# All 16 z blocks in the seven-product pair stage, and the decay of the decode states moved there through DRAM

## The chip, the cores and the metric

The kernel runs on one core of a Trainium2 chip. The metric is the device time of one execution in microseconds. The kernel before has a median of 2105.8 us over 3 runs (2105.5 to 2109.59).

## The reference, cut to what matters

One inference step of a hybrid decoder layer: 1024 tokens of a new prompt, and 8 sequences that are decoded by one token each (T = 1032 columns in the kernel). One input projection gives z, the inputs x, B and C of a state-space mixer (SSD), a pooling input and two gates.

```python
xn = rms_norm(x, p['norm_mix_pre'])
proj = xn @ p['w_in']
z, xbc, dt_raw, u_pool, gate_a, gate_b = jnp.split(proj, idx, axis=-1)
xbc_c, conv_new = causal_conv(xbc, conv_prev, p['conv_w'], p['conv_b'])
xs, bm, cm = jnp.split(xbc_c, [D_INNER, D_INNER + N_GROUPS * D_STATE], axis=-1)
y, ssm_new = ssd_scan(xs, dt, a, bm, cm, ssm_prev)
y = y + p['d_skip'][:, None] * xs
y_a = rms_norm(y * jax.nn.silu(z), p['ssm_norm'])
y_b, pool_new = pool_mix(u_pool, pool_prev, start_pos, p['w_pool_group'], p['pool_scale'])
merged = jax.nn.sigmoid(gate_a) * (y_a @ p['w_branch_a']) + jax.nn.sigmoid(gate_b) * (y_b @ p['w_branch_b'])
h = x + rms_norm(merged @ p['w_out'], p['norm_mix_post'])
gu = rms_norm(h, p['norm_ffn_pre']) @ p['w_ffn_in']
g, up = jnp.split(gu, [D_FF], axis=-1)
f = (jax.nn.silu(g) * up) @ p['w_ffn_out']
out = h + rms_norm(f, p['norm_ffn_post'])
```

For a token of the decoded sequences the scan is one step: the stored state times exp(dt a), plus dt x B, and the output is that state times C. The width of the model is 1024, of z and x 2048 each (16 blocks of 128 rows), and there are 8 groups of SSD heads, each with one block of B, one of C, two of x and two of z.

## The kernel before, in words

Rows of a block lie on the 128 partitions, and tokens along the free axis, in thirds of 344 columns. All products are of float32 quality: each operand is split into a high and a low part, and a product is three matmuls (high by high, high by low, low by high; `mm3`, L260 to L262). The normed input stays on chip as `xh` and `xl`. A weight block comes from DRAM by SP's DMA queue (`wr`), ScalarE casts it to its high part (`wh`, L194), and VectorE subtracts for the low part (`wl`, L195). All weights stand in one plan (`plan_weights`); two loads are kept ahead, and one split is made ahead of its use (`w_dma`, `w_split`, `load_w`). The instructions of each engine are laid out by a scheduler, so their order is not that of the text.

The stages are these. First the pooling branch's projections. Then the **pair stage** (about 146 to 377 us): 22 blocks of the input projection, as 11 pairs, each computed as a product of 2 by 2 blocks in seven products in place of eight. The list `PAIRS` names them: `ga` and `gb` are gate blocks, `z0` to `z3` eight of the 16 z blocks. `prep1` makes the weight operands of a product, three products ahead (`RING`); `product1` runs its 24 matmuls of 258 columns (L710 to L712) and adds the result into rows of the pair (copies L715 and L719, additions L717 to L727). `finish_pair` applies tanh, for z multiplies (L748, L749), and stores the block to DRAM (L750, `s_z`).

Then the **group stage** (about 377 to 1011 us). `group_proj(g)` computes five blocks of group g as direct products: B, C, x0 and x1, each followed by the causal convolution (`conv`: first tap L733 on ScalarE, three taps L735 on VectorE, tanh L736 on ScalarE, multiply L737 on VectorE), and then one z block (`z_proj`, tanh L880 and multiply L881). Beside it runs `ssd(g-1)`, the scan of the group before, in 8 chunks of 128 tokens: per chunk four products into a bank `T` (L916 to L919: transposes of B, x0, x1, and B by C), from which VectorE makes `xdt`, `wx` and `CB` (L924 to L928) and the decay matrix `E` (L935); then the state product into a bank `S` (L948), the state's part of the output (L950), the output product `y` (L960), the state's update `hT` (multiply L967 on GpSimd, addition L968 on VectorE), the state's part times its decay (`eA`, L971), and the sum in `Y` (L976 on VectorE, L980 on GpSimd). Beside the chunks stand the decode steps: load a state (`st`), `dx` (L999), GpSimd's product of B and `dx` (L1001), the decay multiply (L1002), the addition of both (L1006), GpSimd's product with C (L1008), VectorE's reduction (L1012, `ys`). At the end come Y times z (L1033), the store of Y, and the sum of its squares. `interleave` takes 0.585 steps of the SSD to each step of the projection:

```python
    for _ in group_proj(0):
        pass
    for g in range(1, G):
        interleave(group_proj(g), ssd(g - 1), 0.585)
```

The group stage ends with `gates`, beside which the last scan, `ssd(7)`, runs: two gate blocks, then the first quarter of the branch product, whose operand is the stored Y of groups 0 and 1, loaded as `qr` and split into `qh` (ScalarE) and `ql` (VectorE, L1068). The later stages (the rest of the branch products, the output product, the FFN) are not touched by the change.

## Time and profile before

| | before |
|---|---|
| median of 3 runs | 2105.8 us (2105.5 to 2109.59) |
| the profiled execution, its own time | 2109.54 us |
| its span, first to last instruction | 2107.8 us |
| mean granted TensorE clock | 0.991 of full speed |
| TensorE busy | 98% of the span |
| VectorE, ScalarE, GpSimd busy | 69%, 39%, 18% |
| bytes moved by DMA | 256.48 MB, 122 GB/s on average |

A busy share says for which part of the span an engine had an instruction in work. Times of single instructions are those of this one execution. The table by stretches gives the same shares for a part of the span; the lists of groups give the number of instructions of one line and shape, their busy time, the mean length of one, and the idle time of the engine just before them with what ended it; a timeline shows single instructions in order of their start.

### The profile page before, as it was taken

To read this page: it belongs to the slowest core of one execution; us is meant where nothing else is said; L and a number is where in the kernel's file an instruction comes from. 1 tells how busy PE (TensorE), PEld (TensorE's weight loads), DVE (VectorE), ACT (ScalarE), POOL (GpSimd) and SP (SyncE) were. 2 spreads that over 40 slices of the span, in tenths; PEclk is the share of its full clock that TensorE was granted. 3 is DMA by queue.
4 is the path that set the end of the run, shared out by engine and by line. 5 is a ranking of instruction groups with operands and counts; after the bars stand their busy time and mean duration, and the time that the engine had idled before them with its cause. 6 is when DMAs were issued, how large, how long until landed. Compare 5 with 4: busy or idle time off the path is not lost.

```text
span 2107.8 us, 37452 instructions
## 1 busy us (share of the span) xinstructions
PE 2056.8 (98%) x14986; PEld 2031.3 (96%) x14986; DVE 1457.1 (69%) x2455; ACT 825.0 (39%) x1573; POOL 386.6 (18%) x405
## 2 busy tenths in 40 slices
PE   6999999999999999999999999989999999999997
PEld 5999999999999999999999999989999999999997
DVE  7867555468987898887447773769776766654436
ACT  5353433435554555554422024444333323341112
POOL 3100000024345344435100002451000000000004
PEclk9999999999999999999999999989999999999999
DMA  4333332434344444446515454143232222352133
GB/s 168 89 114 96 111 114 90 136 107 154 124 158 155 150 144 149 153 137 221 199 40 165 147 177 132 61 141 116 88 99 71 91 71 81 117 175 71 43 101 109
DMA packets 126574, 256.48 MB, mean 122 GB/s; under 512 B 25408, under 2 KB 63424, under 8 KB 126400
## 3 DMA queue, kind: packets, MB, share of 16 engines
q1 hardware_dynamic: 125968, 253.80, 37.5%
q8 instruction: 118, 1.93, 0.4%
q14 instruction: 56, 0.46, 0.1%
q10 hardware_dynamic: 432, 0.28, 0.0%
HBM read 195.72 MB, written 58.32 MB: 121 GB/s over the span
## 4 chain that ended last, share of the span: by engine, by line
PE 91%; DVE 5%; ACT 1%; issue 1%; POOL 1%; DMA 0%; ACTq 0%; DVEq 0%; POOLq 0%
PE pj L260 22%; PE pj L261 22%; PE pj L262 22%; PE dj L712 3%; PE dj L710 3%; PE dj L711 3%; PE y L960 2%; PE S L948 1%; PE S L950 1%; PE y L260 1%; PE y L262 1%; PE y L261 1%; PE T L260 1%; PE T L262 1%; PE T L261 1%
## 5 line engine op out<-in xcount | busy, mean ns | idle before, releaser
L260 PE MATMUL pj<-xh,wh 128*128 128x344 f32 x1200 | 393.4, 330 | 3.2 <-ACT xh L330 2.4
L261 PE MATMUL pj<-xl,wh 128*128 128x344 f32 x1200 | 385.0, 321 | 0.1
L262 PE MATMUL pj<-xh,wl 128*128 128x344 f32 x1200 | 383.6, 320 | 0.0
L194 ACT CAST wh<-wr 128x1024 fp32r<-128x1024 f32 (+1 forms) x119 | 123.3, 1037 | 386.0 <-PE pj L261 353.8
L260 PEld LDWEIGHTS pj<-xh,wh 128*128 128x128 f32 x1200 | 225.7, 189 | 9.4 <-issue 5.8
L261 PEld LDWEIGHTS pj<-xl,wh 128*128 128x128 f32 x1200 | 226.3, 189 | 1.7 <-DVE xl L331 0.8
L262 PEld LDWEIGHTS pj<-xh,wl 128*128 128x128 f32 x1200 | 226.3, 189 | 0.0
L1198 POOL TENSOR_TENSOR ssacc<-ssacc,sq 128x258 f32<-128x258 f32 (+3 forms) x41 | 42.9, 1051 | 927.5 <-ACT sq L1197 919.3
L195 DVE TENSOR_TENSOR wl<-wr,wh 128x1024 fp32r<-128x1024 f32 (+1 forms) x104 | 132.0, 1270 | 113.3 <-ACT wh L194 102.6
L261 PE MATMUL pj<-ql,wh 128*128 128x344 f32 (+1 forms) x608 | 191.3, 315 | 2.7 <-DVE ql L1068 2.7
L260 PE MATMUL pj<-qh,wh 128*128 128x344 f32 (+1 forms) x608 | 192.2, 316 | 1.4 <-ACT m L1144 1.4
L262 PE MATMUL pj<-qh,wl 128*128 128x344 f32 (+1 forms) x608 | 190.9, 314 | 0.0
L261 PE MATMUL pj<-al,wh 128*128 128x344 f32 (+2 forms) x528 | 169.1, 320 | 0.0
L260 PE MATMUL pj<-ah,wh 128*128 128x344 f32 (+2 forms) x528 | 168.9, 320 | 0.0
L262 PE MATMUL pj<-ah,wl 128*128 128x344 f32 (+2 forms) x528 | 168.8, 320 | 0.0
L735 DVE SCALAR_TENSOR_TENSOR S<-U,hcw,S 128x1056 f32<-128x1056 f32 x96 | 129.6, 1350 | 1.9 <-ACT S L733 1.7
L1453 DVE TENSOR_TENSOR acc<-acc,pj 128x344 f32<-128x344 f32 (+2 forms) x120 | 60.8, 510 | 98.4 <-PE pj L262 98.2
L261 PEld LDWEIGHTS pj<-ql,wh 128*128 128x128 f32 x608 | 115.7, 190 | 2.9 <-DVE ql L1068 2.9
L260 PEld LDWEIGHTS pj<-qh,wh 128*128 128x128 f32 x608 | 115.1, 189 | 2.4 <-ACT m L1144 1.9
L262 PEld LDWEIGHTS pj<-qh,wl 128*128 128x128 f32 x608 | 115.5, 190 | 0.0
L932 ACT ACTIVATE E<-E,acT 128x128 f32<-128x128 f32 x256 | 85.4, 392 | 50.3 <-DMA E<-s_ac 50.3
L261 PEld LDWEIGHTS pj<-al,wh 128*128 128x128 f32 x528 | 99.2, 188 | 0.0
(438 smaller groups left out, 5950.8 us busy)
## 6 DMA issues: line engine op xcount, KB each, us to landing
wr<-wi SPq DMA_DIRECT2D x61, 512.0 KB, 4.0
E<-s_ac SPq DMA_DIRECT2D x64, 256.0 KB, 3.8
wr<-wfi SPq DMA_DIRECT2D x30, 512.0 KB, 3.6
s_act<-wk SPq DMA_DIRECT2D x44, 258.0 KB, 2.0
ar<-s_act SPq DMA_DIRECT2D x22, 516.0 KB, 4.5
wu<-wfi SPq DMA_DIRECT2D x22, 512.0 KB, 3.6
wr<-wfo SPq DMA_DIRECT2D x20, 512.0 KB, 3.6
s_y<-Y SPq DMA_DIRECT2D x16, 516.0 KB, 4.1
```

The lines of the kernel that those rows point to most:

```text
L194: act.copy(out=wh, in_=raw)
L195: eng.tensor_tensor(out=wl, in0=raw, in1=wh, op=ALU.subtract)
L260: pe.matmul(out, wh, xh, start=start, stop=False)
L261: pe.matmul(out, wh, xl, start=False, stop=False)
L262: last_mm[0] = pe.matmul(out, wl, xh, start=False, stop=stop)
L710: pe.matmul(o, wh_, h[:, cs], start=first and k == 0, stop=False, skip_group_check=True)
L711: pe.matmul(o, wh_, l[:, cs], start=False, stop=False, skip_group_check=True)
L712: pe.matmul(o, wl_, h[:, cs], start=False, stop=k == 3, skip_group_check=True)
L735: dve.scalar_tensor_tensor(out=S[:, :CW], in0=U[:, k:k + CW], scalar=tap(k), in1=S[:, :CW], op0=ALU.mult, op1=ALU.add)
L932: act.activation(out=E[:, h], in_=E[:, h], func=AF.Relu, scale=-1.0, bias=acT[:, c, 4 * g + h:4 * g + h + 1])
L1198: eng.tensor_tensor(out=sacc[:, sl], in0=sacc[:, sl], in1=q, op=ALU.add)
L1453: dve.tensor_tensor(out=acc[ob][:, sl], in0=acc[ob][:, sl], in1=pt, op=ALU.add)
```

## The change

Four pairs are added to the pair stage, so that all 16 z blocks are computed there and stored (`s_z` gets a second half). A z pair now holds the same half of two neighbouring groups' z: pairs z0 to z3 the first block of groups 0 to 7, z4 to z7 the second. `z_proj` and `group_proj` fall away, and with them the z weights in the groups' plan; the groups run the four conv blocks alone, and `ssd` loads both z rows. The new generator `decay` loads a decode state, multiplies it by its decay and stores it to DRAM (`s_st`); it is called from the 17th product of the pair stage on, in two of every five steps. `decode` loads the multiplied state and has no multiply. The ratio of `interleave` goes from 0.585 to 0.73. The line numbers of the new kernel are one lower than before up to the pair stage and two higher in the SSD.

```diff
-PAIRS = "ga0 ga1 z0 ga2 z1 ga3 gb0 z2 gb1 z3 gb2".split()
+PAIRS = "ga0 ga1 z0 ga2 z4 ga3 gb0 z1 gb1 z5 gb2 z2 z6 z3 z7".split()
...
         if kind == "z":
-            return WZ + 4 * n + 1, WZ + 4 * n + 3
+            return WZ + 4 * (n % 4) + n // 4, WZ + 4 * (n % 4) + n // 4 + 2
...
-            want(("in", WZ + 2 * g), wi[WZ + 2 * g])
...
-    s_z = dram.tile([G, P, T], F32, name="s_z")
+    s_z = dram.tile([2, G, P, T], F32, name="s_z")
+    s_st = dram.tile([16, P, NS, P], F32, name="s_st")
...
+    def decay(hp):
+        st = row(1024, name="st").rearrange("p (b n) -> p b n", n=P)
+        sync.dma_start(out=st, in_=sssm[hp])
+        yield
+        dve.tensor_tensor(out=st, in0=st, in1=b4x(dts[:, 1, hp * 8:hp * 8 + 8], P), op=ALU.mult)
+        sync.dma_start(out=s_st[hp], in_=st)
+        yield
...
+        if i >= 16 and (i - 16) % 5 in (0, 4):
+            if (i - 16) % 5 == 0 and len(dec) < 16:
+                dec.append(decay(len(dec)))
+            if dec:
+                next(dec[-1], None)
...
-    def z_proj(g):
-        d = grp[g]
-        wt = load_in(WZ + 2 * g)
-        Z = row(name="Z")
-        d["z0"] = Z
-        for th in range(3):
-            pt = yield from in_half(wt, th)
-            act.activation(out=Z[:, TH[th]], in_=pt, func=AF.Tanh, scale=0.5)
-            dve.scalar_tensor_tensor(out=Z[:, TH[th]], in0=Z[:, TH[th]], scalar=1.0, in1=pt,
-                                     op0=ALU.add, op1=ALU.mult)
-            yield
...
-                sync.dma_start(out=v3(st), in_=sssm[hp])
+                sync.dma_start(out=v3(st), in_=s_st[hp])
...
-                dve.tensor_tensor(out=v3(st), in0=v3(st), in1=b4x(dts[:, 1, hp * 8:hp * 8 + 8], P), op=ALU.mult)
...
             if u == 13:
-                d["z1"] = row(name="Z")
-                sync.dma_start(out=d["z1"], in_=s_z[g])
+                for a in range(2):
+                    d[f"z{a}"] = row(name="Z")
+                    sync.dma_start(out=d[f"z{a}"], in_=s_z[a, g])
...
-    for _ in group_proj(0):
+    for _ in conv_proj(0):
         pass
     for g in range(1, G):
-        interleave(group_proj(g), ssd(g - 1), 0.585)
+        interleave(conv_proj(g), ssd(g - 1), 0.73)
```

The new layout moves instructions at three places.

The first is VectorE at the passage from one group to the next, where the last conv of group g (block x1) and the last chunks of `ssd(g-1)` meet. Names: `S` and `U` are the conv's rows (also the bank `S` of the state product in rows of `hT` and `eA`), `pj` a projection bank, `y` the bank of the output product. Before:

```order
L935 TENSOR_TENSOR E<-E,CB 128x512
L737 SCALAR_TENSOR_TENSOR S<-U,S 128x1056
L881 SCALAR_TENSOR_TENSOR Z<-Z,pj 128x344
L968 TENSOR_TENSOR hT<-hT,S 128x256
L971 TENSOR_TENSOR eA<-eA,S 128x2x128
L968 TENSOR_TENSOR hT<-hT,S 128x256
L881 SCALAR_TENSOR_TENSOR Z<-Z,pj 128x344
L971 TENSOR_TENSOR eA<-eA,S 128x2x128
L976 SCALAR_TENSOR_TENSOR Y<-S,ppt,y 128x256 x2
L1033 TENSOR_TENSOR Y<-Y,Z 128x1032 x2
L195 TENSOR_TENSOR wl<-wr,wh 128x1024
L924 TENSOR_TENSOR xdt<-T,dtT 128x256
```

And after the change:

```order
L970 TENSOR_TENSOR hT<-hT,S 128x256
L973 TENSOR_TENSOR eA<-eA,S 128x2x128
L194 TENSOR_TENSOR wl<-wr,wh 128x1024
L735 SCALAR_TENSOR_TENSOR S<-U,hcw,S 128x1056
L978 SCALAR_TENSOR_TENSOR Y<-S,ppt,y 128x256
L735 SCALAR_TENSOR_TENSOR S<-U,hcw,S 128x1056
L978 SCALAR_TENSOR_TENSOR Y<-S,ppt,y 128x256
L735 SCALAR_TENSOR_TENSOR S<-U,hcw,S 128x1056
L1035 TENSOR_TENSOR Y<-Y,Z 128x1032 x2
L737 SCALAR_TENSOR_TENSOR S<-U,S 128x1056
L926 TENSOR_TENSOR xdt<-T,dtT 128x256
L928 TENSOR_TENSOR wx<-T,wend 128x256
```

The conv's last multiply (L737) stood seven rows ahead of the Y by Z pair and now stands behind it, and the conv's taps lie among the last rows of the scan.

The second is TensorE where the scan of group g begins: the transpose of the decode samples (`ident,bcs`) and the four products of the first chunk. Before they stand together, behind the z block:

```order
L262 MATMUL pj<-xh,wl 128x344
L903 MATMUL T<-ident,bcs 16x128
L916 MATMUL T<-ident,S 128x128
L917 MATMUL T<-ident,S 128x128
L918 MATMUL T<-ident,S 128x128
L919 MATMUL T<-S 128x128
L260 MATMUL pj<-xh,wh 128x344
```

After the change they stand in two pieces, the first behind 24 matmuls of the next group's block B, the second 33 such matmuls (32 in the first and the last group) further on:

```order
L261 MATMUL pj<-xh,wl 128x344
L905 MATMUL T<-ident,bcs 16x128
L918 MATMUL T<-ident,S 128x128
L919 MATMUL T<-ident,S 128x128
L259 MATMUL pj<-xh,wh 128x344
```

```order
L261 MATMUL pj<-xh,wl 128x344
L920 MATMUL T<-ident,S 128x128
L921 MATMUL T<-S 128x128
L259 MATMUL pj<-xh,wh 128x344
L260 MATMUL pj<-xl,wh 128x344
```

The transpose of x1 (L920, before L918) thus comes 57 projection matmuls behind the conv block x1's own last matmul, where before it came behind the 72 of the z block.

The third is VectorE near the end of the group stage, where the splits of the first quarter (`ql`) stand among the rows of `ssd(7)`. Before:

```order
L1068 SCALAR_TENSOR_TENSOR ql<-qr,ppt,qh 128x1032
L999 TENSOR_TENSOR dx<-S,dts 128x8
L1002 TENSOR_TENSOR st<-st,dts 128x1024
L968 TENSOR_TENSOR hT<-hT,S 128x256
L971 TENSOR_TENSOR eA<-eA,S 128x2x128
L976 SCALAR_TENSOR_TENSOR Y<-S,ppt,y 128x256 x2
L1006 TENSOR_TENSOR st<-st,tmp 128x1024
L1068 SCALAR_TENSOR_TENSOR ql<-qr,ppt,qh 128x1032 x2
L924 TENSOR_TENSOR xdt<-T,dtT 128x256
```

And after the change:

```order
L1001 TENSOR_TENSOR dx<-S,dts 128x8
L1070 SCALAR_TENSOR_TENSOR ql<-qr,ppt,qh 128x1032
L970 TENSOR_TENSOR hT<-hT,S 128x256
L973 TENSOR_TENSOR eA<-eA,S 128x2x128
L1007 TENSOR_TENSOR st<-st,tmp 128x1024
L978 SCALAR_TENSOR_TENSOR Y<-S,ppt,y 128x256 x2
L1013 TENSOR_REDUCE ys<-tmp 128x8
L1070 SCALAR_TENSOR_TENSOR ql<-qr,ppt,qh 128x1032 x2
L926 TENSOR_TENSOR xdt<-T,dtT 128x256
```

The reduction of the decode product (L1013, before L1012) stood behind the last two splits and now stands ahead of them; the decay multiply (L1002) is gone, and the second split stands behind `dx`.

## Rows read from the trace of the kernel before

**Rows 1.** The page's first part: busy time, share of the span, number of instructions.

```profile
PE 2056.8 (98%) x14986; PEld 2031.3 (96%) x14986; DVE 1457.1 (69%) x2455; ACT 825.0 (39%) x1573; POOL 386.6 (18%) x405
```

**Rows 2.** Table by stretches: window, length, busy us and instructions per engine, clock, DMA, GB/s.

```profile
146.00:377.00 231.00, 228.46 (x1884) 227.64 (x1884) 145.43 (x211) 94.13 (x146) 0.30 (x2) 1.00 0.35 113
315.00:335.17 20.17, 20.17 (x170) 20.17 (x169) 14.55 (x21) 8.32 (x12) 0.00 (x0) 1.00 0.22 79
603.30:676.00 72.70, 72.70 (x512) 70.90 (x511) 61.46 (x91) 38.54 (x84) 31.36 (x35) 1.00 0.46 149
975.60:982.40 6.80, 6.12 (x21) 6.12 (x22) 4.93 (x8) 2.22 (x7) 5.85 (x5) 0.50 0.79 265
```

**Rows 3.** List of TensorE's waits, 377 to 1011 us: us, times, longest.

```profile
PE pj L261 <- DVE ql L1068: 2.7, 1, 2.7
```

**Rows 4.** Timeline of TensorE in the first group's z block: start, us.

```profile
429.10 0.32 PE L262 MATMUL pj<-xh,wl 128*128 128x344 f32 x1
...
437.59 0.32 PE L262 MATMUL pj<-xh,wl 128*128 128x344 f32 x1
```

**Rows 5.** Timeline of ScalarE in the pair stage: the copies after two first products.

```profile
318.84 0.59 ACT L715 COPY gt<-dj 128x516 f32<-128x516 f32 x1 [2.27 <-PE dj L712]
...
339.01 0.59 ACT L715 COPY Z<-dj 128x516 f32<-128x516 f32 x1 [1.10 <-PE dj L712]
```

**Rows 6.** All instructions of line 903: durations, first and last start.

```profile
L903 PE MATMUL T<-ident,bcs x8: 270/271/272, 437.7 to 946.5; 128*16 128x128 f32 x8
```

**Rows 7.** VectorE's groups, 603.3 to 676 us: busy, mean ns, idle before, releaser.

```profile
L735 DVE SCALAR_TENSOR_TENSOR S<-U,hcw,S 128x1056 f32<-128x1056 f32 x12 | 16.2, 1354 | 0.0
L737 DVE SCALAR_TENSOR_TENSOR S<-U,S 128x1056 f32<-128x1056 f32 x5 | 7.6, 1524 | 1.1 <-ACT U L736 1.1
L935 DVE TENSOR_TENSOR E<-E,CB 128x512 f32<-128x512 f32 x8 | 7.4, 920 | 0.1
L195 DVE TENSOR_TENSOR wl<-wr,wh 128x1024 fp32r<-128x1024 f32 x5 | 7.0, 1405 | 4.8 <-ACT wh L194 4.8
...
L924 DVE TENSOR_TENSOR xdt<-T,dtT 128x256 f32<-128x256 f32 x8 | 3.3, 414 | 1.0 <-ACT BT L921 1.0
...
L1033 DVE TENSOR_TENSOR Y<-Y,Z 128x1032 f32<-128x1032 f32 x2 | 2.9, 1486 | 0.5 <-POOL Y L980 0.5
L968 DVE TENSOR_TENSOR hT<-hT,S 128x256 f32<-128x256 f32 x7 | 2.9, 414 | 1.4 <-PE S L950 1.4
...
L1002 DVE TENSOR_TENSOR st<-st,dts 128x1024 f32<-128x1024 f32 x2 | 2.4, 1210 | 0.0
...
L881 DVE SCALAR_TENSOR_TENSOR Z<-Z,pj 128x344 f32<-128x344 f32 x3 | 1.5, 504 | 0.0
...
L1012 DVE TENSOR_REDUCE ys<-bc 128x8 f32<-128x1024 f32 x1 | 1.2, 1222 | 1.6 <-POOL bc L1008 1.6
L1012 DVE TENSOR_REDUCE ys<-tmp 128x8 f32<-128x1024 f32 x1 | 1.2, 1220 | 1.1 <-POOL tmp L1008 1.1
```

**Rows 8.** Timelines of GpSimd and VectorE, 668 to 677 us.

```profile
668.70 2.91 POOL L1001 TENSOR_TENSOR tmp<-bc,dx 128x1024 f32<-128x1024 f32 x1
...
669.77 2.38 DVE L935 TENSOR_TENSOR E<-E,CB 128x512 f32<-128x512 f32 x1
...
676.48 0.68 DVE L935 TENSOR_TENSOR E<-E,CB 128x512 f32<-128x512 f32 x1
```

**Rows 9.** Timeline of GpSimd near the end of the group stage.

```profile
969.03 2.81 POOL L1001 TENSOR_TENSOR bc<-bc,dx 128x1024 f32<-128x1024 f32 x1 [1.91 <-DVE dx L999]
971.81 3.32 POOL L195 TENSOR_TENSOR wl<-wr,wh 128x1024 fp32r<-128x1024 f32 x1
975.09 1.60 POOL L967 TENSOR_TENSOR hT<-hT,cd 128x256 f32<-128x256 f32 x1
...
978.47 2.41 POOL L1008 TENSOR_TENSOR tmp<-st,bc 128x1024 f32<-128x1024 f32 x1
```

**Rows 10.** Timeline of TensorE at the end of its wait there.

```profile
976.28 0.66 PE L261 MATMUL pj<-ql,wh 128*128 128x344 f32 x1 [2.65 <-DVE ql L1068]
```

More of the change, by code (lines that the diff above doesn't have):

```diff
@@ L740, in spots, with b4x @@
         return U[:, SOFF:SOFF + 32].rearrange("p (b k) -> p b k", k=4)
+    def b4x(ap, n):
+        return ap.unsqueeze(2).broadcast_to([P, ap.shape[1], n])
+    def decay(hp):
[5 more added lines that the diff above has]
+        yield
     def finish_pair(name, rs):
@@ L749, in finish_pair @@
                 dve.scalar_tensor_tensor(out=rs[j], in0=t, scalar=1.0, in1=rs[j], op0=ALU.add, op1=ALU.mult)
-                sync.dma_start(out=s_z[2 * n + j], in_=rs[j])
+                sync.dma_start(out=s_z[n // 4, 2 * (n % 4) + j], in_=rs[j])
                 yield
@@ L784, in layer_kernel @@
     tails = []
+    dec = []
     def last_pool(us_):
@@ L813, in layer_kernel @@
             tails.append(finish_pair(name, pair["rows"]))
+        if i >= 16 and (i - 16) % 5 in (0, 4):
[3 more added lines that the diff above has]
+                next(dec[-1], None)
     while tails:
         step_tail()
+    while len(dec) < 16:
+        dec.append(decay(len(dec)))
+        next(dec[-1])
+        next(dec[-1])
     pair.clear()
@@ L871, in conv_proj @@
             yield
-    def z_proj(g):
-        d = grp[g]
-        wt = load_in(WZ + 2 * g)
-        Z = row(name="Z")
-        d["z0"] = Z
-        for th in range(3):
-            pt = yield from in_half(wt, th)
-            act.activation(out=Z[:, TH[th]], in_=pt, func=AF.Tanh, scale=0.5)
-            dve.scalar_tensor_tensor(out=Z[:, TH[th]], in0=Z[:, TH[th]], scalar=1.0, in1=pt,
-                                     op0=ALU.add, op1=ALU.mult)
-            yield
-    def group_proj(g):
-        yield from conv_proj(g)
-        yield from z_proj(g)
-    def b4x(ap, n):
-        return ap.unsqueeze(2).broadcast_to([P, ap.shape[1], n])
     def samples(S):
```

## The prediction

> **What bounds the kernel now.** I read the page's busy shares first: TensorE is busy 98% of the span [rows 1], so only a change in what TensorE executes, or a wait that reaches it, can move the time. A busy share does not say how fast TensorE works, so I go by the spacing of its matmuls below. Next comes the table by stretches, with the pair stage (146 to 377 us) and one steady group (603.3 to 676) [rows 2]. In the steady group TensorE is busy all of 72.70 us and VectorE 61.46 of them, 85%; in the pair stage VectorE is busy 145.43 of 231 us, 63%. The list of waits says that TensorE loses one noteworthy wait in the whole group stage: 2.7 us for a split of SSD output (`ql`) near its end [rows 3]. So the group stage is bound by TensorE's instructions, with VectorE 11.2 us per group behind it, and the change takes work from both.
>
> **Removed and added on TensorE.** One z block in a group is 3 thirds x 8 k x 3 = 72 matmuls of 344 columns. In the first group's z block the two rows shown lie 54 matmuls apart: 437.59 - 429.10 = 8.49 us, 0.157 us each [rows 4], so a block is 11.32 us, and eight are 90.6 us. In the pair stage two blocks take 7 products of 24 matmuls of 258 columns; the copies after the first product of one pair (`gb1`) and of the next (`z3`) are 339.01 - 318.84 = 20.17 us apart [rows 5]. Four more pairs are 80.7 us. So leaving out each pair's eighth product is worth 90.6 - 80.7 = **9.9 us**, 0.47%: a 258-column matmul takes 20.17 / 168 = 0.120 us, 76% of the time for 75% of the columns. This is all that the change can gain from TensorE's instructions.
>
> **The pair stage.** In a pair period that holds a z pair's two finishing multiplies VectorE is busy 14.55 of 20.17 us [rows 2]. The 16 decay multiplies of 1.21 us each [rows 7] come on top: 19.4 us over the last 13 pairs, 1.5 per pair, together 16.1 of 20.17, 80%. I cost them at nothing: weights are prepared three products (8.6 us) ahead, and a PSUM bank is written again only after at least one other product (2.9 us), so one multiply in between is covered; with no cover at all the 16 would be 19.4 us. On SP's queue 16 loads and 16 stores of states and 8 z stores come in, and the stores wait for VectorE in front of weight loads. Two weight loads are ahead of use all the time, about half a pair, and a store is at most a multiply late. Bytes: 16.8 MB of states, 4.2 of weights and 4.2 of z on top of 113 GB/s x 231 us = 26 MB make 51 MB in 312 us, 165 GB/s, against 149 in a steady group where TensorE waits for nothing [rows 2]. Hence 0, with 5 us (a quarter of the uncovered price) as the upper bound. The passage from pairs to groups keeps its order: 0.
>
> **The groups.** Per group VectorE loses three z multiplies (1.5 us), two decay multiplies (2.4) and one weight split (1.4) [rows 7]: 61.46 - 5.3 = 56.1 us. TensorE's period is (946.5 - 437.7) / 7 = 72.68 us [rows 6] and falls by 11.32 to 61.36. VectorE's share then rises from 85 to 91%. What decides is how much of its idle time can go, 11.2 us per group now. The largest piece, 4.8 before a weight split, is VectorE being early: the cast that it waits for waits for TensorE. The other pieces are answers that VectorE waits for inside a chain: 1.1 for the tanh of a conv, 1.0 for the copy after the transposes, 1.4 for the state product, 0.5 for GpSimd's last addition to Y, 1.6 and 1.1 for GpSimd's product before the two reductions [rows 7]; together 6.7. If these stay, VectorE needs 56.1 + 6.7 = 62.8 us for a group, 1.4 more than TensorE.
>
> The order listings show where TensorE would feel it. No z block stands behind group g's x1 conv any more. Before, the last conv multiply stands ahead of the two Y x Z multiplies, and TensorE comes to the transposes of x1 only behind the z block. Now the Y x Z pair, which waits for GpSimd, stands ahead of that conv multiply, and the transpose of x1 comes 57 matmuls, 9.0 us and the SSD's matmuls among them, behind the conv's last matmul. In this time VectorE alone has three taps of 1.35, the Y x Z pair of 2.9 and the last multiply of 1.5 to do, 8.5 us [rows 7], after a cast, a copy and the first tap on ScalarE: about as long as the way. The second place is the state product of the seventh chunk, whose bank VectorE frees last thing in a long row.
>
> Bounds per group: if the waits for tanh, Y and state product are filled (3.0 less) VectorE needs 59.8 and TensorE waits for nothing. If both reductions wait for a whole GpSimd product of 2.41 [rows 9] and get no work ahead of it, 2.7 becomes 4.8, and TensorE waits 3.5. I take 1.4, by which the pieces stay as their rows have them; over the seven groups that run beside an SSD **+10.0**, bounds 0 and +25.
>
> **The end of the group stage.** TensorE's 2.7 us there [rows 3] are a wait for the third `ql` split. Now VectorE's reduction of the decode product stands ahead of that split. Its input comes from GpSimd, behind the product with `dx`, a weight split and a state multiply. Today these start at 969.03 (when `dx` is there) and take 2.81, 3.32, 1.60, then 2.41 for the input [rows 9]. VectorE makes `dx` one 1.28 us split sooner now, so the input is done near 967.8 + 2.8 + 3.3 + 1.6 + 2.4 = 977.9, and a reduction of 1.2 and a split of 1.3 later it is 980.4. Today TensorE goes on at 976.3 [rows 10]: 4.1 us. Against that, the granted clock is half, 1.2 GHz, from 975.6 to 982.4, after today's wait [rows 2], and TensorE would stand still for most of that, which gives back about 2. I take **+2**; bounds -4.5 (the decay multiply's 1.2 gone, and no fall of the clock, 3.3) and +7.5 (a second such stretch).
>
> **Sum.** -9.9 + 10.0 + 2 = +2.1 us against the profiled execution's 2109.5 us: 2111.6. That execution is 3.7 us above the median of the three runs, so on the median's scale it is 2105.8 + 2.1, **2108 us**. About 0.2% (4.2 us) is what a measurement of this kernel can tell from no change: 2101.6 to 2110.0. With the other terms held, the time leaves this band below 0.5 us of waiting per group (faster) and above 1.7 (slower).
>
> **Rivals.**
> *The new order hides the waits (faster).* The instructions were laid out anew on every engine, and TensorE's listing has the x1 transposes moved back by 33 matmuls to where they fit. For it: seven groups pass without a wait of TensorE today, with orders made in the same way [rows 3]. Against it: the idle pieces are latencies that an order does not remove. With 0.2 us per group and an unchanged end: 2105.8 - 9.9 + 1.4 = 2097 us.
> *GpSimd's products set the pace (slower).* VectorE runs longer beside GpSimd: one multiply of E takes 2.38 us beside a GpSimd product of 2.91, another 0.68 [rows 8], the mean is 0.92 [rows 7], so E alone loses 1.9 us per group; and GpSimd's 31.4 us per group [rows 2] now fall into 61 instead of 72.7. The place is the reductions and the Y x Z pair, which wait for GpSimd ahead of instructions that TensorE needs. At 2.5 us per group: 17.5 - 9.9 + 4.1 = 11.7 us. A wait of 2.7 us was followed by 6.8 us at 1.2 GHz [rows 2, 3]; such a stretch costs some 3.4 us, and with one of them the time is 2121 us. It decides from 1.7 us per group. Against it: the mean durations that I used have today's share of this in them. Here I count also the case that the pair stage does not keep 20.17 us.
> The Trainium skill has a rule on this (SBUF — State Buffer, Who interferes with whom): a VectorE instruction with two SBUF inputs and a GpSimd instruction that reads SBUF hold a shared port one at a time, each for its whole length. The trace before agrees: the multiply of 2.38 us ends with the GpSimd product beside it. By that rule the time lost grows with GpSimd's share, 18% here; if all such losses are twice those of E, an estimate, that is 0.7 us per group, +5 in all, and the sum would be 2113 us.
> *The decay does not leave the groups.* The states come back from DRAM already multiplied, so nothing can put the multiply back; a load of the same 512 KB replaces the other. No chance of its own.
>
> **How the numbers follow.** The forecast, no change that can be told, gets 0.40, faster 0.27, slower 0.33. The forecast's own range is 2102 to 2110. The range for 8 in 10 takes in both rivals' times, and leaves out the bound with a clock that does not fall and the far end of the group term: 2096 to 2122.
>
> **What would show it.** Right: pairs still 20.2 us apart and a pair stage of about 312 us; starts of the SSD 62 to 63 us apart instead of 72.7; TensorE waiting 0.5 to 1.7 us per group, for the x1 conv at the transposes and for VectorE's state sum at the seventh chunk; near the end of the group stage one wait of some 6 us for `ql`. A spacing of 61.4 us without waits would prove the faster rival; 64 us and more, with VectorE idle ahead of Y x Z and the reductions, the slower one. A pair spacing over 20.4 us would make the first term wrong.

## The result, and the profile after

The changed kernel takes 2138.34 us (median of 4 runs, 2137.56 to 2140.4), the kernel before 2105.65 beside it: a ratio of 1.0149 (95% interval 1.0137 to 1.0162): **31 to 33 us slower**, 31.4 by the ratio and 32.7 by the medians. The forecast was no change, 2108 us, in a range of 2096 to 2122. The profiled execution took 2140.4 us with a span of 2138.6.

The page's first part, after (busy time, share, instructions), answers to [rows 1]: TensorE is 2 points further from being busy all the time.

```profile
PE 2059.8 (96%) x15082; PEld 2024.1 (95%) x15082; DVE 1499.3 (70%) x2495; ACT 836.6 (39%) x1585; POOL 403.2 (19%) x405
```

The table by stretches, after, with the columns of [rows 2]: the pair stage, the first group, the seven groups that run beside a scan, one of them, and the stretch at half clock near the end of the group stage.

```profile
147.71:459.62 311.91, 309.15 (x2557) 308.36 (x2557) 212.80 (x299) 123.09 (x190) 0.30 (x2) 1.00 0.48 166
459.62:508.76 49.14, 49.14 (x312) 49.08 (x313) 23.76 (x20) 21.74 (x38) 3.69 (x14) 1.00 0.32 94
508.76:975.01 466.25, 443.10 (x3062) 420.62 (x3060) 410.08 (x588) 248.89 (x550) 231.89 (x239) 0.99 0.50 159
706.24:773.85 67.61, 62.84 (x440) 59.39 (x438) 59.66 (x86) 35.91 (x81) 34.70 (x36) 1.00 0.50 158
...
1009.20:1016.00 6.80, 5.93 (x22) 5.87 (x23) 4.37 (x9) 3.04 (x8) 0.61 (x1) 0.50 0.64 202
```

The same table of the kernel before for its pair stage, its first group and its seven groups (not among the rows above):

```profile
146.40:377.28 230.88, 228.46 (x1884) 227.66 (x1885) 145.31 (x212) 93.84 (x146) 0.30 (x2) 1.00 0.35 114
377.28:437.74 60.46, 60.46 (x384) 60.40 (x385) 29.27 (x26) 25.06 (x43) 3.68 (x14) 1.00 0.30 88
437.74:946.51 508.77, 508.77 (x3566) 496.28 (x3563) 429.07 (x629) 264.62 (x579) 216.57 (x240) 1.00 0.46 146
```

Read stage by stage: the pair stage is 81.0 us longer, the first group 11.3 shorter, the seven groups only 42.5 shorter. By TensorE's work alone the seven should be 7 x 11.32 = 79.2 shorter; **36.7 us** are missing. In 23.1 of them (466.25 - 443.10) TensorE stands still. In the other 13.6 it counts as busy but gets no further: a matmul ahead of a stop counts to its modelled end (the timeline below has one), and three stretches run at half clock; by the starts of the matmuls these two make some 10 us. TensorE was busy for all of 508.77 us before, and VectorE left 79.7 us free; now VectorE is busy 410.08 of 466.25, 58.6 us per group.

TensorE's waits after, 508 to 1011 us (us in total, times, longest), to hold against [rows 3]:

```profile
PE S L950 <- DVE eA L973: 17.3, 20, 2.3
PE pj L260 <- DVE ql L1070: 6.2, 1, 6.2
PE S L950 <- ACT E L934: 2.7, 2, 2.2
PE T L920 <- DVE S L737: 2.0, 6, 0.5
```

Most are ended by VectorE's `eA`, which frees the bank of the state product. The starts of the scans ([rows 6]) stand 466.2 / 7 = 66.6 us apart:

```profile
L905 PE MATMUL T<-ident,bcs x8: 271/272/273, 508.8 to 975.0; 128*16 128x128 f32 x8
```

One such wait, in the timelines of VectorE, GpSimd and TensorE, shows what VectorE does meanwhile:

```profile
726.03 0.41 DVE L970 TENSOR_TENSOR hT<-hT,S 128x256 f32<-128x256 f32 x1
726.36 2.27 DVE L937 TENSOR_TENSOR E<-E,CB 128x512 f32<-128x512 f32 x1
728.55 1.66 DVE L737 SCALAR_TENSOR_TENSOR S<-U,S 128x1056 f32<-128x1056 f32 x1
730.14 0.41 DVE L973 TENSOR_TENSOR eA<-eA,S 128x256 f32<-128x256 f32 x1
...
726.19 1.90 POOL L1003 TENSOR_TENSOR bc<-bc,dx 128x1024 f32<-128x1024 f32 x1 [5.78 <-DVE dx L1001]
...
728.28 0.33 PE L261 MATMUL pj<-xh,wl 128*128 128x344 f32 x1
730.69 0.67 PE L950 MATMUL S<-wx,BT 128*128 128x256 f32 x2 [2.09 <-DVE eA L973]
```

Between `hT` and `eA`, which read the same bank, stand a multiply of E that lasts 2.27 us beside a GpSimd product (0.68 when alone, [rows 8]) and a conv's last multiply. The two matmuls start 2.41 us apart, where 0.16 is usual, and the list counts 2.09 as a wait. The groups of VectorE over the seven groups, after, and below them the same of the kernel before (busy, mean ns, idle before):

```profile
L735 DVE SCALAR_TENSOR_TENSOR S<-U,hcw,S 128x1056 f32<-128x1056 f32 x86 | 115.8, 1346 | 1.7 <-ACT S L733 1.6
L937 DVE TENSOR_TENSOR E<-E,CB 128x512 f32<-128x512 f32 x56 | 57.4, 1026 | 1.3 <-ACT E L936 0.9
L737 DVE SCALAR_TENSOR_TENSOR S<-U,S 128x1056 f32<-128x1056 f32 x28 | 43.0, 1534 | 3.8 <-ACT U L736 3.0
L194 DVE TENSOR_TENSOR wl<-wr,wh 128x1024 fp32r<-128x1024 f32 x28 | 42.5, 1518 | 0.4 <-ACT wh L193 0.4
L926 DVE TENSOR_TENSOR xdt<-T,dtT 128x256 f32<-128x256 f32 x56 | 23.2, 415 | 12.9 <-ACT BT L923 12.7
L1013 DVE TENSOR_REDUCE ys<-bc 128x8 f32<-128x1024 f32 x7 | 8.5, 1221 | 14.2 <-POOL bc L1009 14.2
L1013 DVE TENSOR_REDUCE ys<-tmp 128x8 f32<-128x1024 f32 x7 | 8.5, 1220 | 12.9 <-POOL tmp L1009 12.9
L1014 DVE SCALAR_TENSOR_TENSOR Y<-S,ppt,ys 128x8 f32<-128x8 f32 x14 | 7.1, 509 | 0.0
```

```profile
L935 DVE TENSOR_TENSOR E<-E,CB 128x512 f32<-128x512 f32 x56 | 52.4, 936 | 0.5
L195 DVE TENSOR_TENSOR wl<-wr,wh 128x1024 fp32r<-128x1024 f32 x34 | 47.5, 1398 | 34.8 <-ACT wh L194 34.8
L737 DVE SCALAR_TENSOR_TENSOR S<-U,S 128x1056 f32<-128x1056 f32 x28 | 39.8, 1422 | 5.9 <-ACT U L736 5.9
L924 DVE TENSOR_TENSOR xdt<-T,dtT 128x256 f32<-128x256 f32 x56 | 23.2, 414 | 7.3 <-ACT BT L921 7.3
L1012 DVE TENSOR_REDUCE ys<-bc 128x8 f32<-128x1024 f32 x7 | 8.5, 1221 | 10.9 <-POOL bc L1008 10.9
L1012 DVE TENSOR_REDUCE ys<-tmp 128x8 f32<-128x1024 f32 x7 | 8.5, 1220 | 7.7 <-POOL tmp L1008 7.7
L1013 DVE SCALAR_TENSOR_TENSOR Y<-S,ppt,ys 128x8 f32<-128x8 f32 x14 | 3.5, 249 | 0.2
```

The 34.8 us that VectorE stood ahead of TensorE are gone, and its largest waits inside chains grew: 27.1 us at the two reductions (18.6 before), 12.7 at the copy after the transposes (7.3). Each E, each `wl` (counted 28 against 34), each last multiply of a conv and each small addition to Y takes longer on average.

### The profile page after: what moved, and what is told of

It reads as the page before. It is cut to its first block, busy times and chain, and to the rows that moved or that the text cites. A ratio compares the mean times of both kernels' runs of the same rounds, so it can differ in the third digit from the quotient of the medians.

```text
span 2138.6 us, 37881 instructions
## 1 busy us (share of the span) xinstructions
PE 2059.8 (96%) x15082; PEld 2024.1 (95%) x15082; DVE 1499.3 (70%) x2495; ACT 836.6 (39%) x1585; POOL 403.2 (19%) x405
## 4 chain that ended last, share of the span: by engine, by line
PE 49%; DVE 6%; issue 2%; ACT 2%; DMA 1%; POOL 1%; SPq 0%; DVEq 0%; ACTq 0%; POOLq 0%
PE pj L259 13%; PE pj L260 13%; PE pj L261 13%; PE y L259 1%; PE y L261 1%; PE y L260 1%; DVE S L735 1%; PE T L260 1%; PE T L259 1%; PE T L261 1%; DMA E<-s_ac 1%; PE S L260 1%; PE S L259 1%; PE S L261 1%; DMA qr<-s_y 1%
## 5 line engine op out<-in xcount | busy, mean ns | idle before, releaser
L259 PE MATMUL pj<-xh,wh 128*128 128x344 f32 x1008 | 335.0, 335 | 3.6 <-ACT xh L329 2.3
L260 PE MATMUL pj<-xl,wh 128*128 128x344 f32 x1008 | 325.8, 323 | 0.1
L261 PE MATMUL pj<-xh,wl 128*128 128x344 f32 x1008 | 324.8, 322 | 0.0
L193 ACT CAST wh<-wr 128x1024 fp32r<-128x1024 f32 (+1 forms) x111 | 114.8, 1035 | 319.7 <-PE pj L260 283.6
L259 PEld LDWEIGHTS pj<-xh,wh 128*128 128x128 f32 x1008 | 191.8, 191 | 9.7 <-issue 6.2
L260 PEld LDWEIGHTS pj<-xl,wh 128*128 128x128 f32 x1008 | 192.1, 191 | 1.7 <-DVE xl L330 0.8
L261 PEld LDWEIGHTS pj<-xh,wl 128*128 128x128 f32 x1008 | 191.9, 190 | 0.0
L194 DVE TENSOR_TENSOR wl<-wr,wh 128x1024 fp32r<-128x1024 f32 (+1 forms) x96 | 124.5, 1298 | 71.6 <-ACT wh L193 61.1
L735 DVE SCALAR_TENSOR_TENSOR S<-U,hcw,S 128x1056 f32<-128x1056 f32 x96 | 129.0, 1344 | 3.0 <-ACT S L733 2.7
L259 PEld LDWEIGHTS pj<-ah,wh 128*128 128x128 f32 x528 | 99.3, 188 | 0.0
```

The lines of the kernel that those rows point to most:

```text
L193: act.copy(out=wh, in_=raw)
L194: eng.tensor_tensor(out=wl, in0=raw, in1=wh, op=ALU.subtract)
L259: pe.matmul(out, wh, xh, start=start, stop=False)
L260: pe.matmul(out, wh, xl, start=False, stop=False)
L261: last_mm[0] = pe.matmul(out, wl, xh, start=False, stop=stop)
L735: dve.scalar_tensor_tensor(out=S[:, :CW], in0=U[:, k:k + CW], scalar=tap(k), in1=S[:, :CW], op0=ALU.mult, op1=ALU.add)
```

## The experiments

The theory after the result, V: in the groups VectorE, with its waits, is the bound. Its rivals are named in the expectations. "Groups" below means the seven stretches between the starts of the scans: 466.2 us in the changed kernel, and 7 x 61.36 = 429.5 if TensorE waited for nothing.

**Run 1: a second bank for the state product.**

```diff
-    BANKS[0] = {"pj": 3, "T": 2, "S": 1, "y": 2}
+    BANKS[0] = {"pj": 3, "T": 2, "S": 2, "y": 1}
```

> The changed kernel with two PSUM banks for the state product (S) and one for the output product (y), in place of one and two; the order on the engines is the same. Theory V (VectorE is full: 59.7 us of work and 7.9 us of idle time make a period of 67.6 us in the fourth steady group): the waits of TensorE change their place and their sum stays; spacing of the SSD starts 66 to 68 us, time 2133 to 2143. Rival S (the single bank of the state product holds TensorE up, 17.3 us of waits that eA ends, and three half-clock stretches after them): these waits go, spacing 63 to 64, time about 2116.

2138.42 us, groups 467.3. The waits for `eA` are gone, and others stand in their place (list of TensorE's waits, 507 to 975 us):

```profile
PE S L952 <- DVE hT L970: 23.1, 24, 1.6
PE T L920 <- DVE S L737: 6.2, 7, 1.1
```

The bank was where TensorE felt VectorE's lateness, not its cause: rival S falls. The longest waits of the changed kernel, 2.1 to 2.3 us, stand at the third chunk's state product of five groups, not at the seventh, where the expectation of run 2 puts them. And TensorE has its full clock in these groups (1.00, 0.99 in the changed kernel): the stretches at half clock go with the waits, and the groups stay as long without them.

**Run 2: the reductions later.** The call of the third decode step is moved one and two steps back, and a fence puts the reduction behind the last `eA`:

```diff
-            if u in (4, 6, 8, 10, 12, 14):
-                decode(int(u >= 10), (u - 4) // 2 % 3)
+            if u in DEC:      # {4: (0,0), 6: (0,1), 9: (0,2), 10: (1,0), 12: (1,1), 15: (1,2)}
+                decode(*DEC[u])
...
-                dve.reduce_sum(out=ys, in_=v3(tmp), axis=AX.X)
+                with tc.issue_after(last_ea[0].ins):
+                    dve.reduce_sum(out=ys, in_=v3(tmp), axis=AX.X)
```

> The changed kernel with the two reductions of the decode product placed behind the next chunk's E, hT and eA on VectorE, nothing else moved. Theory V: the idle time ahead of the reductions (4.0 us per group) is filled, spacing about 63.5 us, time 2110 to 2116 (28 us less, or less than that by what other idle pieces grow). Rival S: the longest waits of TensorE, at the seventh chunk, have no reduction near them; at most 5 us less, 2133 or more.

2120.68 us, 17.7 less: groups 451.8 (14.4 less) and 3.7 less in the first part of the branch product, where one of these reductions stood ahead of `ql`. V had 28 in the groups alone, and a time of 2110 to 2116: the direction is V's, the size a miss. Five waits of 2.1 to 2.3 us at the third chunk stay. VectorE's rows over the seven groups tell why (first its stretch, then two groups):

```profile
508.60:960.42 451.82, 435.73 (x3061) 417.75 (x3059) 426.64 (x588) 249.87 (x551) 225.69 (x239) 1.00 0.51 165
```

```profile
L937 DVE TENSOR_TENSOR E<-E,CB 128x512 f32<-128x512 f32 x56 | 68.1, 1216 | 3.7 <-ACT E L936 2.6
L194 DVE TENSOR_TENSOR wl<-wr,wh 128x1024 fp32r<-128x1024 f32 x28 | 53.0, 1894 | 1.2 <-ACT wh L193 1.2
L926 DVE TENSOR_TENSOR xdt<-T,dtT 128x256 f32<-128x256 f32 x56 | 23.3, 416 | 14.1 <-ACT BT L923 14.0
```

VectorE's free time fell from 56.2 to 25.2 us, but its busy time rose by 16.6 with the same instructions: E by 10.7 us, `wl` by 10.5, less others. What VectorE now does while GpSimd makes the product lasts longer. `xdt`, which reads one of its operands from PSUM, keeps its 415 ns. So in this run half of the idle time that VectorE gained it lost again by working beside GpSimd.

**Run 3: the decay multiply put back into the groups** (the states are then multiplied twice).

```diff
+                dve.tensor_tensor(out=v3(st), in0=v3(st), in1=b4x(dts[:, 1, hp * 8:hp * 8 + 8], P), op=ALU.mult)
```

> The changed kernel with a second multiply of the loaded decode states by their decay put into the groups' decode (so that the states of the 8 decoded tokens are multiplied twice): two more VectorE instructions of 1.21 us per group. Theory V: spacing 2.4 us longer in each of seven groups, +17 us, 2155. Rival S: the multiply lies in idle time ahead of the reductions, 0 to +5, 2138 to 2143. If GpSimd's chain of products is the bound (rival G), the reductions come 1.2 us later each: also +17.

2145.96 us, groups 473.4: 7.2 us more, above rival S and less than half of the 17 that V and G had. The multiplies take 19.6 us; the waits ahead of the reductions fell from 27.1 to 22.9 us, so part of them lay there, and the small additions to Y from 7.1 to 3.6.

**Run 4: without the additions to the sum of squares.**

```diff
-                pool.tensor_tensor(out=ssacc, in0=ssacc, in1=q, op=ALU.add)
+                pass
```

> The changed kernel without GpSimd's two additions to the sum of squares per group (5.5 us of GpSimd; the sum then holds the first block's squares alone), order of VectorE unchanged. If VectorE's instructions are held up beside GpSimd's (part of theory V), VectorE loses less at the start of each scan: wl and E there shorter, spacing 0.5 to 2 us shorter, 2124 to 2135. Rival S, or no such holding up: spacing unchanged, 2136 to 2140.

2133.88 us, groups 459.1, 1.0 us less per group, with VectorE's order and its waits as they were. Its rows over the seven groups:

```profile
L735 DVE SCALAR_TENSOR_TENSOR S<-U,hcw,S 128x1056 f32<-128x1056 f32 x86 | 123.2, 1433 | 2.6 <-ACT S L733 2.5
L937 DVE TENSOR_TENSOR E<-E,CB 128x512 f32<-128x512 f32 x56 | 49.4, 882 | 2.6 <-ACT E L936 2.3
...
L194 DVE TENSOR_TENSOR wl<-wr,wh 128x1024 fp32r<-128x1024 f32 x28 | 34.0, 1215 | 0.4 <-ACT wh L193 0.4
```

`wl` falls from 1518 to 1215 ns and E from 1026 to 882: GpSimd's work lengthens them. The 16.5 us that the two lose are not all won, for a conv's taps (`L735`), which have two operands in SBUF as well, rise by 7.4; VectorE's busy time falls by 8.7 (410.1 to 401.4).

**Run 5: the decays alone, in the kernel before.** `decay` and its calls as in the change, in two of every four steps from the 13th product on; `z_proj` stays.

> The kernel before with the decay multiplies alone moved into its pair stage, through DRAM (11 pairs, z in the groups as before). Theory V: TensorE waits for nothing in the groups with or without them (72.7 us between starts of the SSD), and the pair stage covers them: 2103 to 2108, the same as before. Rival P (states, stores and multiplies hold the pair stage up): pairs more than 20.2 us apart, up to +19 us, 2110 to 2125.

2110.76 us against 2108.29 beside it, ratio 1.0012 (1.0001 to 1.0022). The groups take 508.65 us, and from the first to the last product of the pair stage 229.73 us pass, as before: rival P falls by its spacing, though the time lies in its range and above V's. The profile shows one longer wait, for `ql` at the end (5.3 us; 2.7 in [rows 3]). In the groups the moved multiplies are worth nothing while TensorE is the bound there. E is longer here than in the changed kernel, though the groups are as long as before:

```profile
L954 DVE TENSOR_TENSOR E<-E,CB 128x512 f32<-128x512 f32 x56 | 68.4, 1221 | 3.8 <-ACT E L953 3.0
```

**Run 6: wx on ScalarE.**

```diff
-            dve.tensor_tensor(out=wx, in0=xv, in1=b4x(wend[:, c, hs], 64), op=ALU.mult)
+            for h in range(R):
+                act.activation(out=wx[:, h], in_=xv[:, h], func=AF.Copy, scale=wend[:, c, 4 * g + h:4 * g + h + 1])
```

> The changed kernel with wx (8 VectorE multiplies of 0.41 us per group) made by ScalarE, four instructions per chunk; the reductions stay where they are. Theory V: VectorE has 3.3 us less per group, spacing about 63.3 us, 23 us less, 2113 to 2119. Rival A (ScalarE's additional 7 us per group come into the chain from transposes to the state product): spacing 66 us or more, 2130 or more.

2131.02 us (two runs, 2127.6 and 2134.4), groups 452.1: 14.1 us less where V had 23, a spacing of 64.6 between V's and rival A's, and a median at the edge of rival A's range. **Run 7, with the late reductions as well:**

> Both: wx on ScalarE and the two reductions behind the next chunk's E, hT and eA. Theory V: 64.5 us per group with the late reductions, less 3.3, is 61.2, about TensorE's 61.4 us: spacing 61.4 to 62.5, 2097 to 2106, and the 9.9 us that the pairs save come out at the end. Rival A: spacing 64 us or more, 2118 or more.

2114.61 us, groups 446.2, between the two expectations. In both runs VectorE now waits for ScalarE (VectorE's waits in run 7, 508 to 975 us):

```profile
DVE CB L931 <- ACT wx L929: 25.3, 27, 1.7
```

`xdt`, `wx` and `CB` read one bank, in this order, and each engine's turn waits for the other's: ScalarE's `wx` waits 36.2 us for `xdt` in run 7. **Run 9** puts wx ahead of `xdt` and `CB` in the code:

> Run 7 with ScalarE's wx ahead of VectorE's xdt and CB in the order in which the three read their bank, so that the bank passes from one engine to the other once per chunk and not three times (in run 7 VectorE waited 25.3 us for wx ahead of CB in seven groups). Theory V: most of these 25 us are VectorE's to use, and TensorE's period nears its own 61.4 us: spacing 62 to 63, 2105 to 2110. Rival A (ScalarE is too late for the chain anyway): the wait comes ahead of xdt in place of CB, spacing 63.5 us or more, 2114 or more.

2111.77 us, ratio 1.0028 (1.0019 to 1.0038), groups 440.8. The wait ahead of `CB` is gone, and 21.7 us of the seven groups stand ahead of `xdt` in its place, as rival A had it: the spacing of 63.0 lies where V had it, the time 2 us above.

**Runs 8 and 10: Y by Z behind the conv's last multiply,** on runs 2 and 9.

```diff
+            with tc.issue_after(conv_last[0].ins):
+                dve.tensor_tensor(out=Y[a], in0=Y[a], in1=d[f"z{a}"], op=ALU.mult)
```

> Run 2 (late reductions) with the two Y by Z multiplies of the scan put behind the last conv multiply of block x1 on VectorE. Theory V: VectorE stays full (64.5 us per group) and TensorE's waits only move from the transposes (1.4 us in all) elsewhere: 2117 to 2123. Rival O (the order at the passage between groups costs by itself, as the prediction's step had it): 1 us or more per group less, 2113 or less.

> Run 9 with the Y by Z multiplies behind the last conv multiply as well. Theory V: with VectorE below TensorE's 61.4 us the 6.5 us of waits at the transposes of x1 (run 7) are worth their length: spacing 61.4 to 62.3, 2098 to 2106, and the kernel is as fast as before or up to 8 us faster. Rival A: 2112 or more.

2125.02 and 2117.97 us: 4 and 6 us worse than runs 2 and 9. Run 8 is a miss for both theories, run 10 for V; it lies where rival A had it. The Y by Z pair had filled the time until the conv's tanh is there. Now VectorE stands still (its waits in run 8; `L738` is the tanh):

```profile
DVE S L739 <- ACT U L738: 20.5, 15, 3.3
```

**Runs 11 and 12: other ratios of interleaving,** 0.66 on the changed kernel, 0.8 on run 9.

> The changed kernel with a ratio of 0.66 SSD steps per projection step in place of 0.73, which lays the scan's instructions out anew on every engine. Theory V (VectorE's work and its waits for GpSimd and ScalarE fill the period): spacing 65.5 to 68 us, 2130 to 2143. Rival D (the layout by 0.73 is what costs): spacing under 64 us, 2115 or less.

> Run 9 (late reductions, wx first, on ScalarE) with a ratio of 0.8. Theory V: VectorE is hardly the bound any more, so what is left (1.6 us per group over TensorE's 61.4) is order: spacing 61.4 to 64, 2102 to 2117, either way. Rival D: as for run 11, 3 us per group or more either way, under 2095 or over 2130.

2131.41 us (groups 462.8) and 2144.10 us (groups 467.6). The first is V's: laying the changed kernel out anew wins 7 us, 3.4 of them in the groups, and not the 23 of rival D. The second is a miss for V and lies where rival D had it: an order alone costs run 9 27 us in the groups. TensorE's waits in run 12, 130 to 1300 us:

```profile
PE T L920 <- DVE S L737: 17.9, 8, 2.9
PE S L951 <- DVE eA L974: 13.4, 9, 2.1
```

So in run 9, where VectorE is idle for 35 of 441 us, one change of order costs more than any single change of VectorE's work or waits has won in these runs.

**Runs 13 and 14: the sum of squares out of the groups,** on runs 2 and 9: `split_quarter` squares each block of Y where the branch product has it on chip again. (In these two runs the sum is taken before the last four blocks are in it.)

```diff
-                pool.tensor_tensor(out=ssacc, in0=ssacc, in1=q, op=ALU.add)
...
+            if 4 * q + j == 0:
+                act.activation(out=ssacc, in_=r_, func=AF.Square)
+            else:
+                act.activation(out=r_, in_=r_, func=AF.Square)
+                pool.tensor_tensor(out=ssacc, in0=ssacc, in1=r_, op=ALU.add)
```

> Run 2 (late reductions) with the sum of squares taken out of the groups: it is formed in the branch product, where Y is loaded again. VectorE's order in the groups is that of run 2. Theory H (VectorE's multiplies with two operands in SBUF are held up beside GpSimd's instructions; in run 2 VectorE's idle time fell by 31 us over seven groups and its busy time rose by 16.6, E by 10.7 and wl by 10.5 of it): GpSimd's 5.4 us per group less give E, wl and the conv's multiplies 1 to 2 us per group back, 451.8 us for seven groups become 439 to 446, 2107 to 2115. Rival O (what is left is the order alone): 450 us or more for seven groups, 2118 or more.

> Run 9 (late reductions, wx first, on ScalarE) with the sum of squares formed in the branch product. Theory H: seven groups take 431 to 436 us in place of 440.8, against 429.5 of TensorE's own work, and the time is 2100 to 2106, between 6 us faster than before and the same. Rival O: 439 us or more, 2110 or more.

Groups 439.1 and 432.6 us, both as theory H had them. VectorE's rows over the seven groups of run 13, with run 2's order:

```profile
L937 DVE TENSOR_TENSOR E<-E,CB 128x512 f32<-128x512 f32 x56 | 60.6, 1081 | 2.5 <-ACT E L936 1.4
L194 DVE TENSOR_TENSOR wl<-wr,wh 128x1024 fp32r<-128x1024 f32 x28 | 47.1, 1684 | 1.9 <-ACT wh L193 1.9
```

E and `wl` together are 13.4 us shorter than in run 2, the groups 12.7. VectorE's busy time falls by only 8.3 (426.6 to 418.3), since the taps grow by 5.0, and its idle time by 4.4 (by 6.1 ahead of `xdt`, where it waits for ScalarE). ScalarE's squares left the groups as well, so this run does not part their share from GpSimd's; run 4 does. Run 13's time, 2112.16 us, is as expected; run 14's, 2110.71 us, is not, and lies in rival O's range: TensorE now waits 6.6 us for `ql` (run 9: 3.0) in the first quarter of the branch product, and 2.6 for an E and 1.5 for an `eA` of the last scan. The wait of 2.8 us for a weight split on GpSimd, which the expectation of run 15 counts here, stands behind the branch product, at 1377.5 us, and in run 9 too (2.75 us).

**Runs 15 and 16: the squares spread over the second and third quarter.**

```diff
+                if qi == 1 or qi == 2:
+                    for _ in range(2):
+                        if sqp:
+                            square(sqp.pop(0), False)
+                if qi == 2 and ob < 2:
+                    for j in range(2):
+                        square(qraw[3][2 * ob + j], True)
+                if qi == 2 and ob >= 2:
+                    ssm_rms((ob - 2) // 2, (ob - 2) % 2)
```

> Run 14 with its 16 squares and 15 additions spread over the second and third quarter of the branch product, not beside the first (all blocks are in the sum when it is taken). Theory H: seven groups take 431 to 434 us as in run 14; the first quarter's waits (5.8 us for ql and 2.8 for a weight split on GpSimd) fall back to about 3; 2099 to 2105, 1 to 7 us faster than before. Rival Q (the squares cost the same wherever they lie in the branch product): 2108 or more.

> Run 13 with the squares spread in the same way. Theory H: seven groups 437 to 441 us as in run 13, time 2107 to 2112, slower than before by 1 to 6 us: without wx on ScalarE VectorE is still over TensorE's 61.4 us per group. Rival Q: 2112 or more.

2107.97 us, ratio 1.0011 (1.0002 to 1.0020), and 2113.62 us. The groups of run 15 are bound by TensorE again; its stretch:

```profile
508.95:942.23 433.28, 431.08 (x3062) 416.62 (x3060) 389.87 (x532) 284.41 (x763) 197.10 (x228) 1.00 0.54 172
```

With 61.9 us per group all but 3.8 of the 36.7 us are won back, and the kernel is still not faster than the one before: run 15 is 3 us above theory H's range, at the border of rival Q's, and run 16 within rival Q's. The place of the squares matters in part: the branch product takes 299.7 us in run 15, 305.7 in run 14 and 296.7 before; the medians of runs 14 and 15 differ by 2.7. But the wait for `ql` is still 5.2 us, so the squares beside the first quarter were only part of its cause. The profiled execution of run 15 is 2.2 us shorter than the one before, but that one lies 3.7 us above its median; the medians decide. Of the versions tried none is faster than the kernel before.

## Why the prediction was wrong

**Removed and added on TensorE: right.** With four more pairs the pair stage is 81.0 us longer (expected 80.7, with pairs 20.17 us apart: two copies after a first product, from the timeline of ScalarE, below), and a z block is 11.32 us in the first group, 60.46 - 49.14. The net gain of 9.9 us is there but for 0.3.

```profile
320.16 0.59 ACT L715 COPY gt<-dj 128x516 f32<-128x516 f32 x1 [2.27 <-PE dj L712]
...
340.33 0.59 ACT L715 COPY Z<-dj 128x516 f32<-128x516 f32 x1 [1.10 <-PE dj L712]
```

**The pair stage: right at 0.** VectorE is busy 212.80 of 311.91 us there, 166 GB/s are moved (estimated 165), and run 5 leaves the pair stage of before as it is to 0.01 us with the 16 multiplies in it.

**The groups: here it failed.** The step was "VectorE needs 56.1 + 6.7 = 62.8 us for a group", and with it the +10.0 us. Measured are 58.6 busy and 8.0 idle, 66.6 us; TensorE's 61.4 leave 5.2 per group, **36.7 us** in place of 10.0, and more than the bound of 25. Two parts were mis-sized.

- The busy time, by 2.5 us. I took the removed instructions off and kept the lengths of the others, and said against the GpSimd rival that "the mean durations that I used have today's share of this in them". They don't keep it. GpSimd has the same instructions per group, and VectorE works beside them more: E +0.7 us per group, `wl` +0.5 (1518 ns in place of 1398), the conv's last multiply +0.5, the small addition to Y +0.5. Run 4 shows for E and `wl` that this is GpSimd: with VectorE's order kept, less GpSimd work makes them shorter. That the shorter period brings the two together, as the forecast's estimate has it, is not shown: run 5, whose period is that of before, has E at 1221 ns (936 before, 1026 after), so which instructions meet is a matter of the order too. The Trainium skill has a rule on this (SBUF — State Buffer, Who interferes with whom): a VectorE instruction contends with GpSimd's reads when both its inputs lie in SBUF, and one with at most one SBUF input, outside the two-port modes, does not. The traces agree, `xdt` stays at 414 to 419 ns and the reduction at 1.2 us in every run. An instruction that is held up waits for the end of the other and then runs: the twelve longest of the 56 multiplies of E after the change end 0.55 to 0.56 us behind the GpSimd instruction during which they began. (The multiply of 2.38 us in rows 8 does so too, 672.15 against 671.61 us, and does not end with the product, as the prediction reads it.) The forecast had this rule as a sum of 2113 us, +0.7 us per group: right in kind, too small.
- The idle pieces, by 1.3 us: the reductions' 2.7 became 3.9, the copy after the transposes' 1.0 became 1.8; the pieces for the tanh and for Y shrank from 1.6 to 0.4. Without the decay multiply ahead of the state's addition VectorE comes to the reductions earlier, and GpSimd does not: that is half of it, for with the multiply back (run 3) they are 3.3.

**The places.** The state product was right, the chunk was not: at the seventh TensorE waits 0.3 to 0.7 us in each group, 4.3 in all, and the longest waits, 2.1 to 2.3 us in five groups, stand at the third, which the forecast does not name (one of them is shown above). The transposes of x1 were not the place: 2.0 us in all, since the Y by Z pair fits into the wait for the tanh; runs 8 and 10, which undo that order, lose 4 and 6 us.

**The end of the group stage: the mechanism was right.** The reduction stands ahead of the `ql` split and waits for GpSimd; TensorE waits 6.2 us in place of 2.7 (forecast 2.7 + 4.1):

```profile
1007.59 1.22 DVE L1013 TENSOR_REDUCE ys<-tmp 128x8 f32<-128x1024 f32 x1 [4.35 <-POOL tmp L1009]
1008.73 2.49 DVE L1070 SCALAR_TENSOR_TENSOR ql<-qr,ppt,qh 128x1032 fp32r<-128x1032 f32 x2
...
1010.07 0.66 PE L260 MATMUL pj<-ql,wh 128*128 128x344 f32 x1 [6.16 <-DVE ql L1070]
```

The 2 us that I gave back for the clock did not come: the stretch at half clock, 1.2 GHz, is again 6.8 us long and begins as before near the end of the wait, so that this part, up to the end of the branch product, cost 4.3 us, not 2. Three more stretches of 3.4 us at half clock followed three of the five waits of 2.1 to 2.3 us in the groups (at 664, 866 and 934 us), a price that the forecast had only in its rival; in run 1, which has none there, the groups are no shorter.

**The sum** by the trace: -9.9 + 36.7 + 4.3 = 31.1, beside a measured difference of 30.8 us between the spans of the two profiled executions (the 0.3 of the pair stage and 1.3 ahead of it come on top, 2.0 behind the branch product go off). So the nearest was the rival "GpSimd's products set the pace", at twice its price (5.2 us per group in place of 2.5), and in part by other means: no idle time stands ahead of Y x Z, and the longer waits ahead of `xdt` are for ScalarE. The chance of 0.33 for slower was too low: rows 7 had the sum of 62.8 above TensorE's 61.4 before any instruction was lengthened.

**What stays open.** How the 5.2 us divide between GpSimd's holding up, the waits and the order can't be said in shares, since each change moves the others: late reductions alone are worth 14.4 us in the groups, GpSimd's additions 7.1 alone, the whole sum of squares 12.7 after the late reductions, and one change of order cost 27. Nor was it tried whether another order would bring run 15 below the kernel before.

## What to carry to other kernels

When work is taken from the bounding engine, add up the next engine's busy time and those of its idle pieces that are answers of others: if they exceed the new period, expect the gain to go, whatever the busy share says: here they made 62.8 us against 61.4, and it came out at 66.6. Idle time of VectorE beside a GpSimd instruction was not free capacity: of 31 us that run 2 filled, 16.6 came back, above all as longer instructions with two operands in SBUF. And a block of matmuls that looks dear (11.3 us direct against 10.1 in the faster scheme) may be the one that hides the other engines' work.

## What the runs showed of the hardware

The length of a VectorE multiply depended on its neighbour on GpSimd more than expected: the mean of the same 28 weight splits was 1215 ns without the additions to the sum of squares (run 4), 1518 in the changed kernel, and 1894 when the reductions no longer kept VectorE waiting (run 2). And a bank that two engines of this program read in turn cost waits at the handovers: VectorE waited 25.3 us for ScalarE between two of its own reads (run 7), and with ScalarE's reads put first (run 9) the groups were 5.4 us shorter, though 21.7 us of waits then stood ahead of VectorE's first read. What of this the chip asks for and what the program's own order, no run here parts.
